# The modulation's row sums on VectorE at their written place in its queue, handed out over the scan and the first MLP

## The chip, the cores and the metric

One Trainium2 chip, and the program runs on 1 of its cores. The metric is the device time of one execution, in microseconds. A core has five engines with a queue each: TensorE (PE, with the weight loads shown as PEld), VectorE (DVE), ScalarE (ACT), GpSimd (POOL), and SyncE (SP), which here only issues transfers. Each queue is worked off in its order; an instruction that waits holds everything behind it in its own queue.

## The reference

A diffusion backbone of two layers over 256 context tokens and 1024 latent tokens, model width 1024. Layer 0 mixes with differential attention beside a bidirectional RWKV-7 recurrence; layer 1 with two other recurrences. What the change touches is the modulation: each layer makes six vectors of 1024 from the conditioning, for the latent tokens and for the context tokens, and uses them around the mixer and around the MLP.

```python
for i in range(DEPTH):
    ...
    m_l = (jax.nn.silu(c) @ mod_w + mod_b)[:, None, :]
    m_c = jax.nn.silu(c_ctx) @ mod_w + mod_b
    ...

def _ada(x, g, shift, scale):
    return rmsnorm(x, g) * (1.0 + scale) + shift

def _sq_relu_mlp(h, w1, w2):
    return jnp.square(jax.nn.relu(h @ w1)) @ w2
```

The six pieces of `m_l` and `m_c` are the shift, scale and gate of the mixer (`sh1`, `sc1`, `g1`) and of the MLP (`sh2`, `sc2`, `g2`). `mod_w` is 1024 x 6144. The vectors made in the stretches below are needed late: `g1` to `g2` of layer 0 after its scan, and layer 1's six not before the end of the first MLP.

## The kernel before

The activations lie with the model width on the 128 partitions: 8 blocks of 128 rows by 1280 tokens. A matrix product of full accuracy is three matmuls (`mm3`, L83 to L85) of a high and a low part of each operand: a weight tile comes in as `wraw`, ScalarE rounds it to `whi` (L91) and GpSimd makes `wlo` (L95).

The stages in order: first normalisation and modulation; the projections of layer 0 with the preparation of the RWKV operands; the **scan** of the RWKV recurrence; the attention heads; the output projection; the **first MLP**; then layer 1 and the second MLP.

**The row sums.** `mods_dot` makes modulation vectors without TensorE. For each vector and each of its 8 blocks of 128 outputs it loads the 128 x 1024 transposed weights (`mdw`, 512 KB, issued on SP at L212, two buffers) and lets VectorE multiply them by the row `silu_r` and add up along the row (L215; `mdj` takes the products, the sum lands in a column of `g1`, `sh2` and so on). Such an instruction is called a dot here. Vectors that the context needs too take two dots for each load. The generator yields after every second load, so a step is 2 loads with 4 dots, or with 2. The scan is handed a generator of 4 vectors with both rows: 16 steps, 32 loads, 64 dots. The first MLP is handed one of 6 vectors, two of them with both rows: 24 steps, 48 loads, 64 dots.

**The scan.** `Rwkv.scan` works through 10 windows of 128 tokens, both directions at once. In each turn `q` of a window it advances several generators by one piece: `window` (the two steps of the recurrence), `back` of the next window (the values and the inverse of the score blocks) and `front` of the window after that (scores and their masks), and hands out a step of the row sums where `q % 3 == 0`. The names in the rows: PE makes scores from `rkr` and `rbk` (L564), VectorE masks them into `rs` (L569), GpSimd cuts blocks out into `imb` (L571). `imc` (L616), shuffles to `imr` (L620), and a chain of products `ipr` (L627) and sums `iuc` (L628) on VectorE invert 8 x 8 blocks; GpSimd writes them to `id` (L632). Then `itt` is a transpose on VectorE (L648, L665), PE multiplies (L652, L658, L672, L683), and VectorE copies results back into `id` under a mask (L660). `iu` (L688) is the finished inverse. The recurrence's step goes PE (L705), `rpm` on VectorE (L708), PE (L711), `sav` on ScalarE and VectorE (L714, L715), PE (L720), the state `S` on VectorE (L724, L725). The projected operands `rkr` and `rbk` are loaded through SP (L553, L554).

**The first MLP.** `up(j)` makes one 128-wide tile of the hidden layer: PE into a bank of PSUM, `relu` on ScalarE (L339), its square on GpSimd (L340), `hidh` and `hidl` on VectorE (L93, L95). `down(c)` multiplies two such tiles by `w2` and adds the result to `x` on VectorE (L364), out of 4 banks `sp` and `ss`. The first three tiles are made in a loop of their own (`first`).

**The order.** The program is written in one order, and the framework's scheduler rearranges each engine's queue when the program is built, by a simulated timeline of its own. So the place of a dot in VectorE's queue need not be that at which it was handed out.

Of the kernel before, what the change touches and what calls it, by code (L numbers as in the profile page):

```python
# [8 lines left out]
F32 = mybir.dt.float32  # L9
# [3 lines left out]
ALU = mybir.AluOpType  # L13
AX = mybir.AxisListType
P = 128
# [11 lines left out]
class Net:  # L27
# [13 lines left out]
    def frame(self, nctx, nt):  # L41

        self.nctx, self.nt = nctx, nt

    @contextmanager
    def pools(self, **kw):
# [151 lines left out]
    def mods_dot(self, pool, rows, bufs, modt, modb, which, names, ctx):  # L198

        nc = self.nc
        outs = [self.const.tile([P, 8, 2], F32, name=nm) for nm in names]

        def steps():
            for (t0, w), o, both in zip(which, outs, ctx):
                if not both:
                    nc.gpsimd.memset(o[:, :, 1:2], 0.0)
                for t in range(8):  # L210
                    raw = pool.tile([P, 1024], F32, name="mdw", tag="mdw", bufs=bufs)
                    nc.sync.dma_start(out=raw, in_=modt[t0 + t])  # L212
                    for j in range(1 + both):
                        junk = pool.tile([P, 1024], F32, name="mdj", tag="mdj", bufs=1)
                        nc.vector.tensor_tensor_reduce(out=junk, in0=raw, in1=rows[:, j], scale=1.0, scalar=modb[:, 8 * w + t : 8 * w + t + 1],  # L215
                                                       op0=ALU.mult, op1=ALU.add, accum_out=o[:, t, j : j + 1])
                    if t % 2:
                        yield
        return outs, steps()
# [104 lines left out]
    def mlp(self, pool, xs, h, w1, w2, gate, groups, aside=iter(()), after=None, wide=None):  # L324


        nc = self.nc
# [41 lines left out]
        for gs in (groups[:-1], groups[-1:]):  # L369
            for w, evict in first:  # L370
                self.proj(w, h, gs, evict)
                next(aside, None)
        for c in range(NH // 2):
            if 0 < c < NH // 2 - 1:
                up(2 * c + 2)
# [7 lines left out]
class Rwkv:  # L383
# [366 lines left out]
    def scan(self, pool, aside):  # L750


        self.pool = pool
        self.half, self.posts = set(), []
        os = [{} for _ in range(12)]
        for g in (self.front(0, os[0]), self.back(os[0]), self.front(1, os[1])):
            for _ in g:
                pass
        self.start(pool)
        for sw in range(10):  # L760
            turn = [self.window(sw, os[sw])] + [self.back(os[sw + 1])] * (sw < 9) + [self.front(sw + 2, os[sw + 2])] * (sw < 8) + self.posts
            self.posts = []
            for q in count():
                turn = [g for g in turn if next(g, 0) is None]
                if not turn:
                    break
                if q % 3 == 0:
                    next(aside, None)

    def post(self, pool, w, d, y, tag):  # L770
# [1142 lines left out]
```

## Time and profile before

| | us |
|---|---|
| median of 3 runs | 4025.93 (4023.85 to 4026.64) |
| the profiled execution, its own time | 4028.34 |
| its span in the trace | 4026.6 |
| granted TensorE clock, mean | 0.929 |

The span is what the trace covers from the first to the last instruction. The clock is given as a share of TensorE's full speed. In the trace every line is that of the kernel before; in the changed kernel the same lines stand 4 further down (dots L220, `rpm` L712).

### The profile page before, as it was taken

To read this page: it belongs to the slowest core of one execution; us is meant where nothing else is said; L and a number is where in the kernel's file an instruction comes from. 1 tells how busy PE (TensorE), PEld (TensorE's weight loads), DVE (VectorE), ACT (ScalarE), POOL (GpSimd) and SP (SyncE) were. 2 spreads that over 40 slices of the span, in tenths; PEclk is the share of its full clock that TensorE was granted. 3 is DMA by queue.
4 is the path that set the end of the run, shared out by engine and by line. 5 is a ranking of instruction groups with operands and counts; after the bars stand their busy time and mean duration, and the time that the engine had idled before them with its cause. 6 is when DMAs were issued, how large, how long until landed. Compare 5 with 4: busy or idle time off the path is not lost. (4 is left out here: it accounts for less than half of the span.)

```text
span 4026.6 us, 69041 instructions
## 1 busy us (share of the span) xinstructions
PE 3604.7 (90%) x28912; PEld 2984.2 (74%) x28912; DVE 2066.0 (51%) x3741; ACT 1139.8 (28%) x1926; POOL 1315.4 (33%) x1121
## 2 busy tenths in 40 slices
PE   6999944777778889899999999999999889999998
PEld 4877833666666667778888887878776777888886
DVE  6354458555567647963333345457237664333335
ACT  3333320121245505111111112574534141111112
POOL 2455532222320015322222223216434353233223
PEclk8999975788889988999999999999989789999999
DMA  5244464223262142541111112222343311111111
GB/s 196 78 132 129 116 207 129 79 81 95 60 190 79 50 144 78 168 136 32 37 42 42 38 36 83 61 84 76 103 126 97 105 51 53 42 53 47 48 42 63
DMA packets 288998, 353.14 MB, mean 88 GB/s; under 512 B 91824, under 2 KB 217264, under 8 KB 288560
## 3 DMA queue, kind: packets, MB, share of 16 engines
q1 hardware_dynamic: 288688, 348.74, 27.8%
q8 instruction: 227, 3.72, 0.4%
q14 instruction: 83, 0.68, 0.0%
HBM read 265.03 MB, written 83.62 MB: 87 GB/s over the span
## 5 line engine op out<-in xcount | busy, mean ns | idle before, releaser
L83 PE MATMUL mm<-acth,whi 128*128 128x512 f32 (+1 forms) x2432 | 903.7, 373 | 26.6 <-ACT acth L91 6.9
L84 PE MATMUL mm<-actl,whi 128*128 128x512 f32 (+1 forms) x2432 | 905.2, 372 | 20.3 <-DVE actl L293 10.7
L85 PE MATMUL mm<-acth,wlo 128*128 128x512 f32 (+1 forms) x2432 | 894.4, 370 | 0.0
L95 POOL TENSOR_TENSOR wlo<-wraw,whi 128x1024 fp32r<-128x1024 f32 (+2 forms) x243 | 500.9, 2067 | 1036.6 <-ACT whi L91 1024.4
L83 PEld LDWEIGHTS mm<-acth,whi 128*128 128x128 f32 x2432 | 467.6, 193 | 122.5 <-issue 8.1
L84 PEld LDWEIGHTS mm<-actl,whi 128*128 128x128 f32 x2432 | 467.5, 192 | 109.0 <-DVE actl L293 11.8
L85 PEld LDWEIGHTS mm<-acth,wlo 128*128 128x128 f32 x2432 | 466.1, 192 | 83.0 <-issue 4.4
L91 ACT CAST whi<-wraw 128x1024 fp32r<-128x1024 f32 (+2 forms) x243 | 217.2, 906 | 994.8 <-PE mm L84 402.6
L340 POOL TENSOR_TENSOR relu<-relu 128x256 f32<-128x256 f32 (+1 forms) x163 | 162.0, 994 | 416.3 <-ACT relu L339 406.7
L93 DVE CAST hidh<-relu 128x256 fp32r<-128x256 f32 (+1 forms) x163 | 72.2, 443 | 366.0 <-POOL relu L340 365.7
L339 ACT ACTIVATE relu<-mm 128x256 f32<-128x256 f32 (+1 forms) x163 | 88.9, 546 | 591.5 <-PE mm L85 421.3
L84 PE MATMUL sp<-hidl,whi 128*128 128x512 f32 (+1 forms) x648 | 238.3, 368 | 1.5 <-DVE hidl L95 1.5
L83 PE MATMUL sp<-hidh,whi 128*128 128x512 f32 (+1 forms) x648 | 238.7, 369 | 0.9 <-DVE x L364 0.9
L85 PE MATMUL sp<-hidh,wlo 128*128 128x512 f32 (+1 forms) x648 | 238.1, 368 | 0.0
L83 PE MATMUL ss<-hidh,whi 128*128 128x512 f32 (+1 forms) x600 | 223.8, 373 | 4.7 <-DVE hidh L93 4.5
L84 PE MATMUL ss<-hidl,whi 128*128 128x512 f32 (+1 forms) x600 | 223.4, 372 | 4.9 <-DVE hidl L95 4.9
L85 PE MATMUL ss<-hidh,wlo 128*128 128x512 f32 (+1 forms) x600 | 222.8, 372 | 0.0
L215 DVE CUSTOM_DVE_ANT_0 mdj<-mdw,silu_r,t_cols 128x1024 f32<-128x1024 f32 x128 | 177.0, 1383 | 36.6 <-DMA mdw<-in_modt_dram 33.1
L364 DVE SCALAR_TENSOR_TENSOR x<-ss,g,x 128x256 f32<-128x256 f32 (+1 forms) x180 | 119.0, 661 | 140.6 <-PE ss L85 140.6
L364 DVE SCALAR_TENSOR_TENSOR x<-sp,g,x 128x512 f32<-128x512 f32 (+1 forms) x192 | 126.6, 660 | 101.7 <-PE sp L85 101.7
L364 DVE SCALAR_TENSOR_TENSOR x<-ss,g2b,x 128x512 f32<-128x512 f32 x120 | 90.0, 751 | 142.3 <-PE ss L85 142.3
L364 DVE SCALAR_TENSOR_TENSOR x<-sp,g2b,x 128x512 f32<-128x512 f32 (+1 forms) x132 | 96.7, 734 | 101.9 <-PE sp L85 101.9
(510 smaller groups left out, 6663.7 us busy)
## 6 DMA issues: line engine op xcount, KB each, us to landing
mdw<-in_modt_dram SPq DMA_DIRECT2D x80, 512.0 KB, 3.6
wraw<-in_wa_dram SPq DMA_DIRECT2D x64, 512.0 KB, 3.6
wraw<-in_wb_dram SPq DMA_DIRECT2D x64, 512.0 KB, 3.5
wraw<-in_win_dram SPq DMA_DIRECT2D x51, 512.0 KB, 3.7
x<-in_xT_dram SPq DMA_DIRECT2D x16, 640.0 KB, 8.5
rw_kr<-rw_t SPq DMA_DIRECT2D x16, 640.0 KB, 3.3
rw_bk<-rw_t SPq DMA_DIRECT2D x32, 320.0 KB, 4.1
rkr<-rw_kr SPq DMA_DIRECT2D x20, 512.0 KB, 5.9
```

The source lines that it names most:

```text
L83: self.nc.tensor.matmul(out, lh, rh, start=start and i == 0, stop=False)
L84: self.nc.tensor.matmul(out, lh, rl, start=False, stop=False)
L85: self.nc.tensor.matmul(out, ll, rh, start=False, stop=stop and i == n - 1)
L91: nc.scalar.copy(out=hi, in_=src)
L93: nc.vector.tensor_copy(out=hi, in_=src)
L95: e.tensor_tensor(out=lo, in0=src, in1=hi.bitcast(F32), op=ALU.subtract)
L215: nc.vector.tensor_tensor_reduce(out=junk, in0=raw, in1=rows[:, j], scale=1.0, scalar=modb[:, 8 * w + t : 8 * w + t + 1], op0=ALU.mult, op ...
L339: nc.scalar.activation(out=r, in_=ps, func=AF.Relu)
L340: nc.gpsimd.tensor_tensor(out=r, in0=r, in1=r, op=ALU.mult)
L364: nc.vector.scalar_tensor_tensor(out=xg, in0=ps, scalar=gate[:, m, j : j + 1], in1=xg, op0=ALU.mult, op1=ALU.add)
```

## The change

The dots are wrapped in `issue_after` of the last VectorE instruction written so far: the scheduler may no longer put a dot ahead of that instruction in VectorE's queue (there is no semaphore in it, only an order). The scan hands out a step where `q % 8 == 4`, which is twice in a window, in place of `q % 3 == 0`. The MLP hands out a step with each `up()` only, and none in the loop over the first three tiles.

```diff
--- before.py
+++ after.py
@@ -41,6 +41,10 @@
     def frame(self, nctx, nt):
 
         self.nctx, self.nt = nctx, nt
+
+    def last(self, engine):
+
+        return next(i for i in reversed(self.nc.cur_bb.bb.instructions) if i.engine == engine)
 
     @contextmanager
     def pools(self, **kw):
@@ -210,10 +214,11 @@
                 for t in range(8):
                     raw = pool.tile([P, 1024], F32, name="mdw", tag="mdw", bufs=bufs)
                     nc.sync.dma_start(out=raw, in_=modt[t0 + t])
-                    for j in range(1 + both):
-                        junk = pool.tile([P, 1024], F32, name="mdj", tag="mdj", bufs=1)
-                        nc.vector.tensor_tensor_reduce(out=junk, in0=raw, in1=rows[:, j], scale=1.0, scalar=modb[:, 8 * w + t : 8 * w + t + 1],
-                                                       op0=ALU.mult, op1=ALU.add, accum_out=o[:, t, j : j + 1])
+                    with self.tc.issue_after(self.last(mybir.EngineType.DVE)):
+                        for j in range(1 + both):
+                            junk = pool.tile([P, 1024], F32, name="mdj", tag="mdj", bufs=1)
+                            nc.vector.tensor_tensor_reduce(out=junk, in0=raw, in1=rows[:, j], scale=1.0, scalar=modb[:, 8 * w + t : 8 * w + t + 1],
+                                                           op0=ALU.mult, op1=ALU.add, accum_out=o[:, t, j : j + 1])
                     if t % 2:
                         yield
         return outs, steps()
@@ -369,7 +374,6 @@
         for gs in (groups[:-1], groups[-1:]):
             for w, evict in first:
                 self.proj(w, h, gs, evict)
-                next(aside, None)
         for c in range(NH // 2):
             if 0 < c < NH // 2 - 1:
                 up(2 * c + 2)
@@ -764,7 +768,7 @@
                 turn = [g for g in turn if next(g, 0) is None]
                 if not turn:
                     break
-                if q % 3 == 0:
+                if q % 8 == 4:
                     next(aside, None)
 
     def post(self, pool, w, d, y, tag):
```

**VectorE at the start of the scan.** Before, in the chain of products and sums of the first inverse (a dot is a row `ISA mdj`, the small `ISA` row behind it reads its sum out):

```order
L215 ISA mdj,g_4226<-mdw,silu_r,t_cols_66 128x1024
L215 ISA g_4226 128x1
L627 TENSOR_TENSOR ipr<-iuc,imr 128x16x2
L215 ISA mdj,g_4226<-mdw,silu_r,t_cols_66 128x1024
L215 ISA g_4226 128x1
L628 TENSOR_REDUCE iuc<-ipr 128x16
L215 ISA mdj,g_4226<-mdw,silu_r,t_cols_66 128x1024
L215 ISA g_4226 128x1
L627 TENSOR_TENSOR ipr<-iuc,imr 128x16x3
L215 ISA mdj,g_4226<-mdw,silu_r,t_cols_66 128x1024
L215 ISA g_4226 128x1
L628 TENSOR_REDUCE iuc<-ipr 128x16
```

After, the same chain:

```order
L631 TENSOR_TENSOR ipr<-iuc,imr 128x16x2
L632 TENSOR_REDUCE iuc<-ipr 128x16
L631 TENSOR_TENSOR ipr<-iuc,imr 128x16x3
L632 TENSOR_REDUCE iuc<-ipr 128x16
L631 TENSOR_TENSOR ipr<-iuc,imr 128x16x4
L632 TENSOR_REDUCE iuc<-ipr 128x16
L631 TENSOR_TENSOR ipr<-iuc,imr 128x16x5
```

The dots between the chain's steps are gone from here; no dot stands ahead of the scan's first `rpm`.

**VectorE in a window of the scan, between the last scores and the second step's `rpm`.** Before, behind the last two `rs`:

```order
L569 TENSOR_TENSOR rs_5327<-rw,t_masks_85 128x512
L569 TENSOR_TENSOR rs_5330<-rw,t_masks_85 128x512
L708 TENSOR_TENSOR rpm<-rbv,rw 128x512
L660 COPY_PREDICATED id<-t_masks_85,rw 128x16x16
L665 STREAM_TRANSPOSE itt<-id 128x512
L715 TENSOR_SCALAR sav_4365<-rw 64x512
L677 TENSOR_SCALAR iwt<-rw 32x512
```

After:

```order
L573 TENSOR_TENSOR rs_5303<-rw,t_masks_85 128x512
L573 TENSOR_TENSOR rs_5306<-rw,t_masks_85 128x512
L220 ISA mdj,g_4226<-mdw,silu_r,t_cols_66 128x1024
L220 ISA g_4226 128x1
L220 ISA mdj,g_4226<-mdw,silu_r,t_cols_66 128x1024
L220 ISA g_4226 128x1
L712 TENSOR_TENSOR rpm<-rbv,rw 128x512
L220 ISA mdj,g_4226<-mdw,silu_r,t_cols_66 128x1024
L220 ISA g_4226 128x1
L220 ISA mdj,g_4226<-mdw,silu_r,t_cols_66 128x1024
L220 ISA g_4226 128x1
```

Two dots moved in ahead of `rpm`, and two between `rpm` and the masked copy into `id` and its transpose.

**VectorE in the same window, the chain of the inverse.** Before, from `iu` on, and at the chain's end:

```order
L688 COPY iu<-rw 32x16x32
L627 TENSOR_TENSOR ipr<-iuc,imr 128x16x3
L628 TENSOR_REDUCE iuc<-ipr 128x16
L627 TENSOR_TENSOR ipr<-iuc,imr 128x16x4
L628 TENSOR_REDUCE iuc<-ipr 128x16
```

```order
L627 TENSOR_TENSOR ipr<-iuc,imr 128x16x6
L628 TENSOR_REDUCE iuc<-ipr 128x16
L627 TENSOR_TENSOR ipr<-iuc,imr 128x16x7
L628 TENSOR_REDUCE iuc<-ipr 128x16
L627 TENSOR_TENSOR ipr<-iuc,imr 128x128
L628 TENSOR_REDUCE iuc<-ipr 128x16
L648 STREAM_TRANSPOSE itt<-id 128x512
L708 TENSOR_TENSOR rpm<-rbv,rw 128x512
```

After, the same two places:

```order
L692 COPY iu<-rw 32x16x32
L220 ISA mdj,g_4226<-mdw,silu_r,t_cols_66 128x1024
L220 ISA g_4226 128x1
L631 TENSOR_TENSOR ipr<-iuc,imr 128x16x3
L220 ISA mdj,g_4226<-mdw,silu_r,t_cols_66 128x1024
L220 ISA g_4226 128x1
L632 TENSOR_REDUCE iuc<-ipr 128x16
```

```order
L220 ISA g_4226 128x1
L632 TENSOR_REDUCE iuc<-ipr 128x16
L631 TENSOR_TENSOR ipr<-iuc,imr 128x16x5
L632 TENSOR_REDUCE iuc<-ipr 128x16
L631 TENSOR_TENSOR ipr<-iuc,imr 128x16x6
L632 TENSOR_REDUCE iuc<-ipr 128x16
L631 TENSOR_TENSOR ipr<-iuc,imr 128x16x7
L632 TENSOR_REDUCE iuc<-ipr 128x16
L712 TENSOR_TENSOR rpm<-rbv,rw 128x512
L631 TENSOR_TENSOR ipr<-iuc,imr 128x128
L632 TENSOR_REDUCE iuc<-ipr 128x16
L652 STREAM_TRANSPOSE itt<-id 128x512
```

Four dots moved in between `iu` and the chain's second sum from there, and `rpm` moved up ahead of the chain's last product and sum and of the transpose `itt`. Eight windows out of the ten have a group of four dots at the one place, and eight at the other.

**VectorE in the first MLP.** Before, near the start of the MLP, among the operands of the first hidden tiles (`act` is the normalised input):

```order
L215 ISA mdj,sh1b<-mdw,silu_r,t_cols_68 128x1024
L215 ISA sh1b 128x1
L95 TENSOR_TENSOR hidl<-relu,hidh 128x512
L215 ISA mdj,sh1b<-mdw,silu_r,t_cols_68 128x1024
L215 ISA sh1b 128x1
L293 TENSOR_TENSOR actl<-adat,acth 128x512
L215 ISA mdj,sh1b<-mdw,silu_r,t_cols_68 128x1024
L215 ISA sh1b 128x1
L93 CAST hidh<-relu 128x256
```

After, the dots handed out first stand further on, among the additions to `x` of the first `down()`:

```order
L99 TENSOR_TENSOR hidl<-relu,hidh 128x512
L220 ISA mdj,sh1b<-mdw,silu_r,t_cols_68 128x1024
L220 ISA sh1b 128x1
L369 SCALAR_TENSOR_TENSOR x_14437<-ss,g_4229,x_14437 128x512
L220 ISA mdj,sh1b<-mdw,silu_r,t_cols_68 128x1024
L220 ISA sh1b 128x1
L369 SCALAR_TENSOR_TENSOR x_14437<-sp,g_4229,x_14437 128x512
L369 SCALAR_TENSOR_TENSOR x_14438<-ss,g_4229,x_14438 128x256
L220 ISA mdj,sh1b<-mdw,silu_r,t_cols_68 128x1024
L220 ISA sh1b 128x1
L369 SCALAR_TENSOR_TENSOR x_14438<-sp,g_4229,x_14438 128x512
```

A dot now stands behind each of a few additions, four with a step; later steps have two.

On SP the loads of `mdw` moved with the dots: 2 behind the scan's preparation, then in each window two ahead of the loads of `rbk` and `rkr`, one behind them and one further on; in the MLP two behind each weight tile. On the other engines the order is the same but for single instructions.

## Rows read from the trace of the kernel before

**Rows 1.** The page: the span; busy time of each engine with its share of the span and its instructions; the dots as the page groups them (busy us, mean ns | idle time of VectorE just before them, and what ended most of it).

```profile
span 4026.6 us, 69041 instructions
PE 3604.7 (90%) x28912; PEld 2984.2 (74%) x28912; DVE 2066.0 (51%) x3741; ACT 1139.8 (28%) x1926; POOL 1315.4 (33%) x1121
L215 DVE CUSTOM_DVE_ANT_0 mdj<-mdw,silu_r,t_cols 128x1024 f32<-128x1024 f32 x128 | 177.0, 1383 | 36.6 <-DMA mdw<-in_modt_dram 33.1
```

**Rows 2.** The dots by their tile: shortest, median and longest in ns, and the start of the first and of the last in us.

```profile
L215 DVE CUSTOM_DVE_ANT_0 mdj<-mdw,silu_r,t_cols x128: 1237/1284/3412, 549.3 to 1768.1; 128x1024 f32<-128x1024 f32 x128
```

**Rows 3.** Busy time by stretch (us from the span's start): length; busy us and instructions of PE, PEld, DVE, ACT, POOL; granted clock; DMA share; GB/s. The first is from the first dot of the scan to its first `rpm`, the second lies in it; the third is the scan's first window and the fourth a later one, each from an `rpm` to the same one of the next window; the last two lie in the first MLP.

```profile
549.34:678.05 128.71, 43.52 (x956) 37.41 (x954) 99.55 (x175) 9.98 (x17) 29.89 (x25) 0.59 0.62 194
600.00:650.00 50.00, 9.93 (x573) 9.22 (x575) 43.59 (x78) 1.19 (x2) 6.67 (x5) 0.50 0.52 163
678.05:739.39 61.34, 37.40 (x1104) 33.66 (x1104) 36.33 (x96) 8.22 (x14) 12.51 (x17) 0.69 0.20 63
876.59:921.13 44.54, 33.02 (x1104) 29.75 (x1104) 22.87 (x54) 8.18 (x14) 9.50 (x14) 0.81 0.23 74
1600.00:1800.00 200.00, 180.40 (x864) 149.15 (x863) 166.20 (x247) 28.03 (x38) 61.89 (x34) 0.95 0.47 150
1800.00:2000.00 200.00, 200.00 (x1036) 170.15 (x1035) 76.40 (x129) 25.24 (x36) 56.07 (x38) 1.00 0.14 43
```

**Rows 4.** The dots alone in the first and third of these stretches: length; busy us and count on VectorE; clock; DMA share; GB/s.

```profile
549.34:678.05 128.71, 77.60 (x59) 0.59 0.62 194
678.05:739.39 61.34, 6.48 (x5) 0.69 0.20 63
```

**Rows 5.** VectorE's timeline at the start of the scan: start, duration, line, operation, tiles, and in brackets the idle time before it and what ended it.

```profile
581.09 1.28 DVE L215 CUSTOM_DVE_ANT_0 mdj<-mdw,silu_r,t_cols 128x1024 f32<-128x1024 f32 x1 [11.51 <-DMA mdw<-in_modt_dram]
586.60 1.98 DVE L616 TENSOR_REDUCE imc<-imb 128x128 f32<-128x1024 f32 x1 [0.61 <-POOL imb L571]
...
617.98 0.70 DVE L648 STREAM_TRANSPOSE itt<-id 128x512 f32<-128x512 f32 x1
...
631.35 0.42 DVE L660 COPY_PREDICATED id<-t_masks,rw 128x256 f32<-128x256 int32 x1
...
646.00 0.42 DVE L660 COPY_PREDICATED id<-t_masks,rw 128x256 f32<-128x256 int32 x1
...
678.05 0.68 DVE L708 TENSOR_TENSOR rpm<-rbv,rw 128x512 f32<-128x512 f32 x1
```

**Rows 6.** PE's timeline there: the products whose results the two masked copies take, and the last product of that inverse.

```profile
623.41 1.81 PE L658 MATMUL rw<-id,iwt 32*32 32x32 f32 x115 [1.44 <-issue]
...
637.05 1.81 PE L658 MATMUL rw<-id,iwt 32*32 32x32 f32 x115 [0.33 <-issue]
...
651.04 0.31 PE L683 MATMUL rw<-id,iwt 32*32 32x32 f32 x2 [0.74 <-ACT iwt L679]
```

**Rows 7.** VectorE's timeline in the later window, one without dots.

```profile
897.27 1.29 DVE L569 TENSOR_TENSOR rs<-rw,t_masks 128x512 f32<-128x512 f32 x2 [4.92 <-PE rw L564]
898.48 0.68 DVE L708 TENSOR_TENSOR rpm<-rbv,rw 128x512 f32<-128x512 f32 x1
...
902.01 0.44 DVE L660 COPY_PREDICATED id<-t_masks,rw 128x256 f32<-128x256 int32 x1 [2.85 <-PE rw L658]
902.48 0.71 DVE L665 STREAM_TRANSPOSE itt<-id 128x512 f32<-128x512 f32 x1
...
908.59 2.02 DVE L616 TENSOR_REDUCE imc<-imb 128x128 f32<-128x1024 f32 x1 [1.11 <-POOL imb L571]
...
918.20 0.27 DVE L628 TENSOR_REDUCE iuc<-ipr 128x16 f32<-128x112 f32 x1
...
920.39 0.71 DVE L648 STREAM_TRANSPOSE itt<-id 128x512 f32<-128x512 f32 x1 [1.27 <-POOL id L632]
921.13 0.69 DVE L708 TENSOR_TENSOR rpm<-rbv,rw 128x512 f32<-128x512 f32 x1
...
924.60 0.69 DVE L715 TENSOR_SCALAR sav<-rw 64x512 f32<-64x512 f32 x1 [1.58 <-ACT sav L714]
```

**Rows 8.** PE's timeline in that window: what stands behind the transpose of 902.48, behind the `rpm` of 921.13 and behind the `sav` of 924.60.

```profile
903.53 1.20 PE L672 MATMUL rw<-itt,rs 32*32 32x32 f32 x64
...
921.97 1.65 PE L711 MATMUL rw<-rpm,iu 64*64 64x64 f32 x26 [3.58 <-DVE rpm L708]
...
926.26 0.48 PE L720 MATMUL rw<-sav,rbt 128*64 128x64 f32 x2
```

**Rows 9.** GpSimd's timeline: a pair of blocks cut out at the start of the scan, with dots on VectorE, and in the later window, without.

```profile
583.06 3.50 POOL L571 TENSOR_TENSOR imb<-rs,t_masks 64x256 f32<-64x256 f32 x2 [12.47 <-DVE rs L569]
...
898.04 1.52 POOL L571 TENSOR_TENSOR imb<-rs,t_masks 64x256 f32<-64x256 f32 x2 [8.38 <-DVE rs L569]
```

**Rows 10.** What PE waited for from 1590 to 1770 us, the first stretch of the first MLP: us in total, times, longest.

```profile
PE mm L83 <- ACT relu L339: 5.0, 3, 3.1
PE ss L84 <- DVE hidl L95: 4.9, 2, 2.7
PE ss L83 <- DVE hidh L93: 4.5, 1, 4.5
```

**Rows 11.** SP's timeline and PE's in the later window: the loads of `rkr` for the window after next, and the scores that read them.

```profile
909.30 1.04 SPq L553 DMA_DIRECT2D rkr<-rw_kr  x2
...
916.30 2.08 PE L564 MATMUL rw<-rkr,rbk 64*128 64x128 f32 x16 [0.72 <-DVE iuc L628]
```

## The prediction, made before the changed kernel was run

> **What bounds the kernel now.** The page first: PE is busy for 90% of the span and VectorE for 51%, and all 128 dots together take 177 us of VectorE [rows 1]. So in most of the program VectorE's work lies beside PE's, and a dot's place can matter only where PE waits. The dots' own range, 549 to 1768 us [rows 2], says where to look, and the table by stretch shows two such places. At the start of the scan, from the first dot to the first `rpm`, PE is busy for 43.5 of 128.7 us while VectorE is busy for 99.6 [rows 3], 77.6 of them with 59 dots [rows 4]. In the first MLP PE loses 19.6 of the first 200 us, at a clock of 0.95, and then nothing at all at 1.00 [rows 3]. Between the two lies the scan, where a later window takes 44.5 us with PE busy for 33.0, VectorE for 22.9 and GpSimd for 9.5: there no engine is full, and the time is that of a chain that goes back and forth between PE and VectorE. So the reader should see two stretches in which the bunches of dots stand in the way, and, between them, windows now free of dots that will get eight each.
>
> **The change part by part.** The order shows the dots out of the scan's start, in two groups of four in each of eight windows, and in the MLP behind the first hidden tiles. Work is neither added nor removed. A dot takes 1.28 us in the median [rows 2] and 1.38 in the mean [rows 1]; I use 1.30 where nothing is in its way.
>
> *The start of the scan.* Four pieces of the one chain of the first inverse.
> (a) VectorE stood for 11.51 us until 581.09 for a dot's load, with masked scores queued behind it, and the dot took 1.28 [rows 5]: 12.8 goes.
> (b) From `imc` to the first `itt` took 31.4 us (586.60 to 617.98), with a dot between nearly all steps [rows 5]; the same chain took 11.8 in the later window (908.59 to 920.39) [rows 7]: 19.6 goes.
> (c) PE had the results for the two masked copies at 625.22 and 638.86 [rows 6], VectorE took them at 631.35 and 646.00 [rows 5]. The copies were 6.1 and 7.1 late, in a queue of dots; in the later window the copy waited for PE [rows 7]: 13.3 goes.
> (d) From the last product of the inverse at 651.04 [rows 6] to the first `rpm` at 678.05 [rows 5] is 27.0 us with 13 dots, 17 at 1.30 each. What part PE's own work covers the rows don't tell. Nothing goes at the least, 17 at the most; I take 9, half.
> The sum is −55. Bounds: −46 without (d), −63 with the whole of it.
>
> *The scan's first window.* It has 5 dots at its head, 6.5 us [rows 4], and takes 16.8 us more than the later one; 4.4 of that is PE's own work being slower (37.4 against 33.0 busy, clock 0.69 against 0.81) [rows 3], which may stay. The other 12.4 goes: −12, bounds −6.5 (the dots alone) and −16.8. Its new group of dots is counted next.
>
> *The windows.* No window of before has dots in these places, so I walk through the later one.
> First group: two dots ahead of the second step's `rpm`, two behind it. Masked scores end at 898.5; two dots put `rpm` at 901.1, and two more, to 904.4, the copy that now goes at 902.01 after 2.85 us of waiting [rows 7]. PE's next product, at 903.53 [rows 8], moves with the transpose: +2.4.
> Second group: four dots, 5.2 us, in the chain of the inverse. The sum at 918.20 ends at 923.7, and `rpm`, now directly behind it, goes there and not at 921.13; then come the last product and sum, GpSimd's 1.27, the transpose, and `sav`, at about 927.6 and not at 924.60 [rows 7]. PE waits for that `rpm` already (3.58) and for `sav` behind it [rows 8]. Between the 2.5 of `rpm` and the 3.0 of `sav` I take 2.5.
> With the 0.1 by which the mean dot is above the median for each of eight dots that makes 5.7 a window, and +46 for eight. Bounds: +19 if only one group costs its 2.4, +83 if each dot costs its 1.30.
> One thing in the trace bears on that 0.1: a pair of cuts on GpSimd took 3.50 us beside dots and 1.52 without [rows 9], so the two engines are in each other's way. [...]
>
> *The MLP.* Its first 200 us lose 19.6 in idle time, and the clock of 0.95 costs 5% of 180.4, 9.0: 28.6 in all [rows 3]. PE waited there 4.9 for `hidl` and 4.5 for `hidh`, VectorE's work behind dots, and 5.0 for `relu` on ScalarE [rows 10]. The `relu` wait is not the dots', and I leave 5 for it. The new places cost something too: the 64 dots go over some hundreds of us in which PE now waits for nothing and VectorE is busy for 38% [rows 3], beside additions that have PSUM banks to spare, so nothing for most; I put 5, four dots that meet a hidden tile. −18, bounds −4 (9.4 for `hidl` and `hidh`, less 5) and −28.6.
>
> *SP.* A load of `mdw` now stands ahead of the loads of `rkr` in each window. A dot of the first group frees its buffer by 904.4, and `rkr` goes out at 909.30 behind a load that waits for PE: nothing, with the price in the rivals.
>
> Sum: −55 −12 +46 −18 = −39. The profiled execution took 4028.3, so 3989; it lay 2.4 above the median, so **3987**.
>
> **The rivals.** A measurement of this kernel can tell about 0.2%, 8 us, from no change.
> *A, the dots hide in the scan too.* For it: VectorE is idle for half of a window. Against: PE waits for `rpm` directly behind the dots [rows 8]. One us a window, the MLP keeping 25: −55 −12 +8 −25 = −84, 3942.
> *B, each dot costs its own time in the windows.* For it: the scan is one chain, and both groups stand on it. Against: the first copy has 2.85 us of slack. With +83 the sum is −2, 4024; with the scan's start at its lower bound too, 4033.
> *C, the other side: the clock.* PE's clock follows how busy it is: 0.50 where PE worked 9.9 of 50 us, 0.69 in the slow first window, 0.81 in the later ones, 1.00 in the full MLP [rows 3]. If windows with dots fall to the first one's state, each takes 16.8 more, +134 over eight: −55 −12 +134 −18 = +49, 4075. It decides from 11 us a window. Against it: a window 6 us longer is nearer to 44.5 than to 61.3, and keeps PE's gaps about as short. [...]
> *D, the loads.* `rkr` is issued at 909.30 and read from 916.30 on [rows 11], with little to spare. If the loads of `mdw` ahead of it hold it back by that whole distance, 7.0 a window, that is +56 and a sum of +17, 4043. Against it: the buffers are free 5 us earlier.
> That the change moves nothing is excluded by the order.
>
> **How the numbers follow.** Chances: the forecast 0.68, A 0.10, B 0.14, C 0.05, D 0.03. The forecast's own range is 3954 to 4018, from about half of each bound taken together. The range of 3945 to 4030 holds it, the upper half of A and most of B; what it leaves out is half of A, C, D and the end of B, 0.17. Faster (below 4018) has the forecast, A and a fifth of B: 0.81. Same has three fifths of B: 0.09. Slower has C, D and the rest: 0.10.
>
> **What would show it.** In the changed kernel the first `rpm` comes some 55 us earlier, near 623, and the first masked copies go when PE's product ends. Windows with dots take about 50 us at a clock of at least 0.77, with PE waiting longer for `rpm` and for the transposes; about 45 would be A, 55 B, 60 at 0.70 C. PE's waits for `rkr` would stand out under D. In the MLP the waits for `hidh` and `hidl` are gone, and PE stays above 195 of 200 us after the first hidden tiles. The prediction is wrong if a window costs 10 us or more, or if the scan's start keeps its length because the loads of `rkr`, PE's slow clock or GpSimd set it in place of the dots.

## The result and the profile of the changed kernel

The changed kernel takes 3971.7 us in the median of 4 runs (3967.53 to 3980.13), the kernel before in the same comparison 4024.9: a ratio of 0.9873, with a 95% interval of 0.9853 to 0.9894. That is 53 us less, where 38 were forecast (3987, range 3945 to 4030). The same kernel came to 3970.4 and 3966.1 in two later comparisons, 56 and 59 below the kernel before on the same chip.

The page first: the span (61 less than in [rows 1], since the profiled execution of before lay 2.4 above its median and this one 4.2 below), and the dots, whose wait for a load is gone. (In the changed kernel the lines from the dots to the first MLP stand 5 further down, not 4: the dots at L220, `relu` at L344.)

```profile
span 3965.7 us, 68983 instructions
L220 DVE CUSTOM_DVE_ANT_0 mdj<-mdw,silu_r,t_cols 128x1024 f32<-128x1024 f32 x128 | 172.7, 1349 | 1.2
```

The dots by their tile, as in [rows 2]: they now run from 645 to 2275 us, and not from 549 to 1768.

```profile
L220 DVE CUSTOM_DVE_ANT_0 mdj<-mdw,silu_r,t_cols x128: 1271/1280/2014, 644.9 to 2274.7; 128x1024 f32<-128x1024 f32 x128
```

Busy time by stretch, with the columns of [rows 3]: from the same instant to the first `rpm`; the scan's first window; the second, the fourth and the fifth; and the first MLP's first two stretches of 200 us.

```profile
549.34:617.65 68.31, 39.15 (x958) 34.13 (x956) 25.30 (x57) 10.20 (x18) 16.73 (x25) 0.68 0.48 143
617.65:671.68 54.03, 34.71 (x1104) 31.16 (x1104) 38.30 (x100) 8.22 (x14) 10.76 (x15) 0.78 0.27 87
671.68:724.00 52.32, 35.61 (x1104) 32.08 (x1104) 33.83 (x70) 8.21 (x14) 13.85 (x16) 0.76 0.42 129
777.29:830.90 53.61, 34.01 (x1106) 30.47 (x1104) 36.38 (x79) 8.22 (x14) 12.08 (x15) 0.82 0.39 126
830.90:879.01 48.11, 32.48 (x1104) 29.29 (x1104) 32.66 (x70) 8.18 (x14) 10.36 (x14) 0.85 0.36 112
1545.00:1745.00 200.00, 199.39 (x1020) 169.93 (x1020) 113.42 (x192) 43.97 (x64) 60.32 (x43) 0.97 0.17 51
1745.00:1945.00 200.00, 200.00 (x1033) 169.90 (x1032) 103.39 (x176) 26.46 (x38) 60.77 (x39) 1.00 0.27 85
```

Three things are to be seen. The scan's start takes 68.3 us and not 128.7, with nearly the same work on PE (39.2 against 43.5 busy, at a higher clock). The windows, 44.5 in the one of [rows 3], are now 48 to 54. And PE is full at the beginning of the MLP, busy for 199.4 of 200 us where it had 180.4, although VectorE still has dots there in the second stretch (103 busy against 76).

VectorE at the start of the scan, to be held against [rows 5]: no dot, and the instructions wait for PE instead of being waited for.

```profile
574.40 1.98 DVE L620 TENSOR_REDUCE imc<-imb 128x128 f32<-128x1024 f32 x1 [1.04 <-POOL imb L575]
...
584.82 0.71 DVE L652 STREAM_TRANSPOSE itt<-id 128x512 f32<-128x512 f32 x1 [1.20 <-POOL id L636]
590.76 0.42 DVE L664 COPY_PREDICATED id<-t_masks,rw 128x256 f32<-128x256 int32 x1 [5.23 <-PE rw L662]
...
597.60 0.43 DVE L664 COPY_PREDICATED id<-t_masks,rw 128x256 f32<-128x256 int32 x1 [5.68 <-PE rw L662]
...
617.65 0.68 DVE L712 TENSOR_TENSOR rpm<-rbv,rw 128x512 f32<-128x512 f32 x1
```

PE there, as in [rows 6]:

```profile
588.40 2.31 PE L662 MATMUL rw<-id,iwt 32*32 32x32 f32 x128 [0.80 <-ACT iwt L657]
...
601.76 0.31 PE L687 MATMUL rw<-id,iwt 32*32 32x32 f32 x2 [0.74 <-ACT iwt L683]
```

VectorE in the fifth window, which answers to [rows 7]: first the group of dots around the second step's `rpm`, then the one in the chain of the inverse, up to the next window's `rpm`.

```profile
850.85 1.37 DVE L220 CUSTOM_DVE_ANT_0 mdj<-mdw,silu_r,t_cols 128x1024 f32<-128x1024 f32 x1
...
852.26 1.62 DVE L220 CUSTOM_DVE_ANT_0 mdj<-mdw,silu_r,t_cols 128x1024 f32<-128x1024 f32 x1
...
853.82 0.68 DVE L712 TENSOR_TENSOR rpm<-rbv,rw 128x512 f32<-128x512 f32 x1
...
856.94 0.44 DVE L664 COPY_PREDICATED id<-t_masks,rw 128x256 f32<-128x256 int32 x1
857.42 0.71 DVE L669 STREAM_TRANSPOSE itt<-id 128x512 f32<-128x512 f32 x1
...
871.09 0.69 DVE L692 COPY iu<-rw 32x512 f32<-32x512 f32 x1
871.81 1.28 DVE L220 CUSTOM_DVE_ANT_0 mdj<-mdw,silu_r,t_cols 128x1024 f32<-128x1024 f32 x1
...
878.71 0.27 DVE L632 TENSOR_REDUCE iuc<-ipr 128x16 f32<-128x112 f32 x1
879.01 0.69 DVE L712 TENSOR_TENSOR rpm<-rbv,rw 128x512 f32<-128x512 f32 x1
```

What PE waited for in the scan from the first to the last `rpm` (617 to 1089 us), the two lines that changed most (total, times, longest):

```profile
PE rw L715 <- DVE rpm L712: 49.0, 14, 6.9
PE rw L676 <- DVE itt L669: 15.2, 8, 2.6
```

The same wait for `rpm` in the kernel before, from 678 to 1118 us:

```profile
PE rw L711 <- DVE rpm L708: 30.0, 8, 5.1
```

The product of L676 (L672 there) has no wait for the transpose `itt` in that kernel. So the windows pay at the places of the walk: at `rpm`, and at the transpose behind the first group's dots.

Where the 61 us between the two profiled executions lie, by the marks in the traces (first and last `rpm`, the first `relu`, the MLP's first and last product with `hidh`, the second MLP's last one):

| stretch, us | before | changed | difference | forecast |
|---|---|---|---|---|
| start to the first `rpm` | 678.1 | 617.6 | −60.4 | −55 |
| first to last `rpm` of the scan | 440.2 | 471.9 | +31.6 | −12 +46 = +34 |
| to the first MLP's first `relu` | 451.5 | 456.4 | +4.9 | 0 |
| first `relu` to the end of the first MLP | 933.9 | 905.0 | −28.9 | −18 |
| layer 1 with the second MLP | 1498.8 | 1490.6 | −8.2 | 0 |

### The profile page after: what moved, and what is told of

It reads as the page before. It is cut to its first block, busy times and chain, and to the rows that moved or that the text cites. A ratio compares the mean times of both kernels' runs of the same rounds, so it can differ in the third digit from the quotient of the medians.

```text
span 3965.7 us, 68983 instructions
## 1 busy us (share of the span) xinstructions
PE 3587.8 (90%) x28912; PEld 2976.9 (75%) x28912; DVE 2048.2 (52%) x3741; ACT 1138.8 (29%) x1926; POOL 1305.6 (33%) x1121
## 4 chain that ended last, share of the span: by engine, by line
PE 58%; DVE 3%; DMA 1%; ACT 1%; issue 1%; POOL 0%; SPq 0%; POOLq 0%; ACTq 0%; DVEq 0%
PE mm L87 10%; PE mm L88 10%; PE mm L89 10%; PE ss L87 4%; PE ss L88 4%; PE ss L89 4%; PE sp L88 4%; PE sp L87 4%; PE sp L89 4%; PE sp L1222 1%; PE ss L1475 1%; PE sp L1406 1%; PE si L1491 1%; PE mm L1232 1%; DMA wraw<-in_wout_dram 0%
## 5 line engine op out<-in xcount | busy, mean ns | idle before, releaser
L344 ACT ACTIVATE relu<-mm 128x256 f32<-128x256 f32 (+1 forms) x163 | 88.9, 545 | 520.8 <-PE mm L89 378.7
L369 DVE SCALAR_TENSOR_TENSOR x<-ss,g,x 128x256 f32<-128x256 f32 x180 | 118.9, 661 | 145.2 <-PE ss L89 145.2
L220 DVE CUSTOM_DVE_ANT_0 mdj<-mdw,silu_r,t_cols 128x1024 f32<-128x1024 f32 x128 | 172.7, 1349 | 1.2
## 6 DMA issues: line engine op xcount, KB each, us to landing
x<-in_xT_dram SPq DMA_DIRECT2D x16, 640.0 KB, 10.7
```

What stands on the lines that cost most here:

```text
L344: nc.scalar.activation(out=r, in_=ps, func=AF.Relu)
L369: nc.vector.scalar_tensor_tensor(out=xg, in0=ps, scalar=gate[:, m, j : j + 1], in1=xg, op0=ALU.mult, op1=ALU.add)
```

## The experiments

The theory: the bunches cost at the scan's start and in the MLP what the chain of the first inverse and the hidden tiles waited for them; the windows pay for what the dots add to the waits of the chain between PE and VectorE; the three add up. The rivals: each dot costs its own time wherever it stands, the windows' longer time is not the dots' but the clock's or the loads', or one part is the whole gain.

One part of the change needs no run. With the new rates alone, without the order edge, the scheduler builds the queues of all five engines row by row as those of before: the rates by themselves do nothing.

**The scan's part alone.** The MLP keeps its old hand-outs and has no edge.

```diff
-    def mods_dot(self, pool, rows, bufs, modt, modb, which, names, ctx):
+    def mods_dot(self, pool, rows, bufs, modt, modb, which, names, ctx, pin=True):
...
-                    with self.tc.issue_after(self.last(mybir.EngineType.DVE)):
+                    with self.tc.issue_after(self.last(mybir.EngineType.DVE)) if pin else nullcontext():
...
             for w, evict in first:
                 self.proj(w, h, gs, evict)
+                next(aside, None)
...
+                ("sh1b", "sc1b", "g1b", "sh2b", "sc2b", "g2b"), (True, True, False, False, False, False), pin=False)
```

> The scan's dots as in the changed kernel, the first MLP's as before. The two profiles put the scan's start at -60.4 (first rpm at 617.65 and not 678.05) and the rest of the scan at +31.6 (first to last rpm 471.9 and not 440.3). Sum theory (the parts add up): 29 below the kernel before, about 3996, with the first MLP's idle time unchanged. Rival, the change of the MLP is the whole gain, and the scan gives back what it gained: within 8 of the kernel before. Rival, the scan alone makes the whole gain and the MLP only moves with the clock: 53 below.

Measured: 4005.6, 21 below the kernel before (ratio 0.9946, 0.9926 to 0.9967), 8 short of the theory's 29, which lies within the interval (13 to 30 below). The profiled execution is its fastest, 3992.8; there the first `rpm` is at 616.4, the scan takes 475.0, and the MLP 932.7 as before, so that the scan's part is 27. Both rivals fall: it is neither nothing nor the whole.

**The MLP's part alone.** The same flag at the scan's call, and `q % 3 == 0` there.

> The first MLP's dots as in the changed kernel, the scan's as before. Sum theory: 29 below the kernel before (first relu to the MLP's last product 933.2 us before and 904.3 after in the two profiles), about 3996; PE busy above 208 of the first 210 us. Rival: the MLP's part is that of the start only, 19.6 us of idle time, with the clock unchanged: 15 to 20 below.

Measured: 3991.2, 35 below (0.9915, 0.9896 to 0.9934). The scan is as before (first `rpm` at 681.5, then 440.0), and the MLP takes 903.7 and not 933.9. The two parts come to 21 + 35 = 56 where the whole change has 53 to 59: they add up. The rival with the start alone falls, since the MLP is 30 shorter and not 15 to 20.

**A kernel that was to have no dots in the scan.**

> The changed kernel without the 64 dots and 32 loads of the scan: layer 0's g1, sh2, sc2 and g2 are left at zero, so the output is another. It prices the dots at their new places. Sum theory (the walk through a window, 5 to 6 us for eight dots): 40 to 46 below the changed kernel, about 3928, windows of 45 us. Rival, each dot costs its own 1.30 us: 83 below, about 3889. Rival, they hide: within 10 of the changed kernel, 3962 or more.

The edit added an argument that nothing read, so this was the changed kernel once more, with all its dots. It prices nothing; as a repetition it gave 3970.4, with 471.7 from first to last `rpm`.

**The scan without its dots.**

```diff
         outs = [self.const.tile([P, 8, 2], F32, name=nm) for nm in names]
+        if skip:
+            for o in outs:
+                nc.gpsimd.memset(o, 0.0)
+            return outs, iter(())
```

> The changed kernel without the 64 dots and 32 loads of the scan (layer 0's g1, sh2, sc2 and g2 stay zero, so the output is another). The scan from its first to its last rpm took 440 before, 472 in the changed kernel and 447 with the four places. Sum theory: the windows lose 40 to 46 to the changed kernel and the first one is near the others without its old 5 dots, so 426 to 432 from first to last rpm, and 40 to 46 less time than the changed kernel. Rival, each dot costs its own 1.30 us in the chain: 83 less, 389. Rival, the dots are hidden in the changed kernel and its longer windows come from another cause, the clock or the loads: 465 or more.

Measured: 3925.8 (0.9750 of before, 0.9735 to 0.9765), 40 to 46 less than the changed kernel's 3966 to 3972. From first to last `rpm` it takes 429.8. So the 64 dots with their 32 loads cost 42.0 us, where the dots themselves are 83 long, in the changed kernel's windows; PE's waits for the loads of `rkr` there are 1.3 to 4.6 us in three profiles of that kernel, so the loads themselves hold PE up by little. Against the kernel before it is 10.4 less (440.2 to 429.8), and that is the first window without its old 5 dots: 50.2 and not 61.3. Both rivals fall. What the 42.0 is made of is seen in the same table by stretch, first to last `rpm`, without dots:

```profile
619.30:1049.10 429.80, 312.59 (x10175) 277.24 (x10176) 234.57 (x600) 87.45 (x158) 112.31 (x142) 0.85 0.25 75
```

and in the changed kernel:

```profile
617.65:1089.50 471.85, 329.16 (x10176) 294.12 (x10176) 317.80 (x730) 87.70 (x159) 127.17 (x145) 0.79 0.33 102
```

The same 10,176 matmuls are busy for 16.6 us longer at a clock of 0.79 and not 0.85; the other 25.4 is idle time of PE. So some two fifths of the price is matmuls that take longer at a lower clock. The idle time is at the two places named above: without dots PE waits for `rpm`

```profile
PE rw L719 <- DVE rpm L716: 31.8, 8, 5.0
```

which is 17 less than in the changed kernel, and the 15.2 for the transpose is gone; the two are more than the 25.4, since other waits are shorter with the dots. The price is uneven: window by window the first eight take 1.3 to 9.2 us more with dots than without, and the fifth, whose timeline is shown above, is the cheapest.

**Four other places in the window.** Two dots at a time, in the first four turns of each of eight windows.

```diff
-                    if t % 2:
+                    if (t + 1) % every == 0:
                         yield
...
+                                                  [(8 * q, 2 + q) for q in range(4)], ("g1", "sh2", "sc2", "g2"), (True,) * 4, every=1)
...
-                if q % 8 == 4:
+                if q in (0, 1, 2, 3):
                     next(aside, None)
```

> The changed kernel with the scan's dots handed out two at a time, in the first four turns of a window. The order then has them at four places, behind the masked scores, behind sav, ahead of the masked copy and at the first transpose, where VectorE waited for PE for 1.6 to 4.9 us in a window without dots, and none in the chain of the inverse. Theory, a dot costs what it adds to PE's wait for rpm, and nothing in a wait of VectorE: windows of 46 to 48 us, 20 to 35 below the changed kernel, about 3945. Rival, the window pays for VectorE's time wherever it stands: within 8 of the changed kernel. Rival, the loads of mdw ahead of rkr hold up the scores: above the changed kernel, with PE waiting for a load.

Measured: 3936.9 (0.9780, 0.9760 to 0.9799), 33 below the changed kernel beside it; 3938.9 when it was repeated on another chip (0.9789, 0.9768 to 0.9810). It is faster than both kernels of this study. The scan takes 447.1 from first to last `rpm`: the 64 dots cost 17.3 us and not 42.0. PE waits for no load of `rkr` there, so both rivals fall. The stretch in the columns of the table above:

```profile
617.43:1064.49 447.06, 324.85 (x10175) 289.71 (x10176) 321.14 (x728) 87.26 (x158) 127.90 (x142) 0.80 0.35 108
```

Against the kernel without dots PE is idle for only 5.0 us more (122.2 and 117.2); the other 12.3 is its matmuls at 0.80 and not 0.85. VectorE's timeline in a window of it, from the first step's `rpm` to the second's and the next window's:

```profile
908.13 0.69 DVE L712 TENSOR_TENSOR rpm<-rbv,rw 128x512 f32<-128x512 f32 x1
...
909.94 1.37 DVE L220 CUSTOM_DVE_ANT_0 mdj<-mdw,silu_r,t_cols 128x1024 f32<-128x1024 f32 x1
...
911.35 1.63 DVE L220 CUSTOM_DVE_ANT_0 mdj<-mdw,silu_r,t_cols 128x1024 f32<-128x1024 f32 x1
...
913.74 1.28 DVE L220 CUSTOM_DVE_ANT_0 mdj<-mdw,silu_r,t_cols 128x1024 f32<-128x1024 f32 x1
...
920.46 1.63 DVE L220 CUSTOM_DVE_ANT_0 mdj<-mdw,silu_r,t_cols 128x1024 f32<-128x1024 f32 x1
...
922.02 0.41 DVE L664 COPY_PREDICATED id<-t_masks,rw 128x256 f32<-128x256 int32 x1
922.35 1.27 DVE L220 CUSTOM_DVE_ANT_0 mdj<-mdw,silu_r,t_cols 128x1024 f32<-128x1024 f32 x1
...
932.32 0.69 DVE L712 TENSOR_TENSOR rpm<-rbv,rw 128x512 f32<-128x512 f32 x1 [0.56 <-PE rw L709]
...
953.44 0.69 DVE L712 TENSOR_TENSOR rpm<-rbv,rw 128x512 f32<-128x512 f32 x1
```

This window has eight dots (three of them left out here) and takes 45.3 us, 0.8 more than the one without any in [rows 3]; it is one of the shorter ones, the eight take 45.2 to 53.3, on average 48.7, where 46 to 48 was expected. The second `rpm` waits for PE (0.56), so the dots ahead of it have lost nothing that counts; the chain of the inverse behind it has no dot, and so the next `rpm` comes 21.1 later (22.7 in [rows 7]). That bears the theory out as far as waits go: the 64 dots add 5.0 us to PE's idle time in places where VectorE waits for PE, and 25.4 in the places of the changed kernel, where PE waits for VectorE. The last pair, at the first transpose, is the weak place: PE's waits for that transpose are 13.9, and 5.7 without dots, which shorter waits elsewhere make good in part.

**The edge with the old rates.** `q % 3 == 0` in the scan and the hand-outs in the MLP's first loop put back, the edge kept.

> Dots kept at their written place, but handed out at the old rates: all 64 of the scan in its first three windows, about 20 a window, and those of the MLP from its first tiles on. Theory, VectorE's waits in a window take some 8 dots and the rest lies on the chain: three windows cost 55 to 75 us together, the scan's start stays at 617, the MLP gains 20 to 29; sum 10 to 35 below the kernel before, 15 to 45 above the changed kernel. Rival, the rates make no difference once the place is kept: within 8 of the changed kernel.

Measured: 3987.9 (0.9911, 0.9893 to 0.9929), 40 below the kernel before, a little more than the 10 to 35 expected, and 16 to 22 above the changed one. The first `rpm` is at 615.5, so the start needs the edge alone; the scan takes 487.7, 57.9 more than without dots, 57 of it in its first three windows, within the 55 to 75 forecast. The MLP takes 913.9. The rates matter once the place is kept.

**The hand-outs in the MLP's first loop put back**, in the changed kernel otherwise.

```diff
             for w, evict in first:
                 self.proj(w, h, gs, evict)
+                next(aside, None)
```

> The changed kernel with the hand-outs in the loop over the MLP's first three tiles put back: six steps, 24 dots, 31 us of VectorE in the 50 us in which PE first waits for hidden tiles. Theory, these dots stand ahead of hidh and hidl: from the first relu to the first down 53 to 60 and not 50, the whole 3 to 10 above the changed kernel. Rival, VectorE has the time: within 3 by the stretch, no difference in the whole.

Measured: 3985.0 and, on the chip of the changed kernel's repetition, 3979.1; both are 13 above the changed kernel, more than the 3 to 10 expected, and the runs are scattered (3971 to 4001, and 3969 to 3992). In the profile of the repetition the stretch to the first `down` is 53.5 and not 50.1, the rest of the MLP 862.3 and not 855.0, and PE waits at its beginning for a hidden tile (1540 to 1760 us):

```profile
PE ss L87 <- DVE hidh L97: 5.9, 1, 5.9
```

In the changed kernel that wait was 0.4 (1545 to 1755 us):

```profile
PE ss L87 <- DVE hidh L97: 0.4, 1, 0.4
PE ss L88 <- DVE hidl L99: 0.2, 1, 0.2
```

So dropping these hand-outs is worth 10.7 by the stretches, and 7.9 in the first profile (51.6 and 861.4).

**A second choice of places.** As the four, with turn 4 in the place of turn 3.

```diff
-                if q in (0, 1, 2, 3):
+                if q in (0, 1, 2, 4):
```

> As the four places, with the fourth pair not ahead of and behind the first transpose but ahead of the second step's rpm. In the four places a half window from the first to the second rpm took 26.1 and not 24.0: sav is late by about 1.0 behind the first pair, and the transpose by 1.3 behind a dot. Theory: the second of these goes, and rpm has 3 us to spare at its new neighbour: 1.0 and not 2.3 a window, 8 to 12 below the four places, about 437 from first to last rpm. Rival, the dots ahead of rpm are on the chain: 2.6 a window in the place of 1.3, 10 above the four places.

Measured: 3954.9 (0.9821, 0.9805 to 0.9838). The scan is the shorter by 4.3, 442.8, less than the 8 to 12 forecast, and for another reason. The wait for the first transpose did shrink, from

```profile
PE rw L656 <- DVE itt L652: 13.9, 7, 4.8
```

with the four places to

```profile
PE rw L656 <- DVE itt L652: 8.5, 6, 4.8
```

but other waits grew, and PE's idle time as a whole is 5.3 longer (127.5 and 122.2). What makes the scan shorter is the matmuls, 9.5 us less at a clock of 0.83 and not 0.80:

```profile
615.82:1058.62 442.80, 315.35 (x10175) 280.58 (x10176) 324.55 (x728) 87.73 (x159) 134.54 (x142) 0.83 0.35 109
```

Yet the whole is 18 longer than with the four places. The excess lies outside the scan, where the two kernels' code is the same. Four kernels on one chip, each run in 5 rounds, were to settle that.

> The changed kernel once more, on one chip with the next three. Both theories below: 50 to 56 below the kernel before.

> The four places once more. Their scan is 4 longer than with the second choice of places (447 and 443 from first to last rpm), but the whole was 18 shorter in another call, 11 of it between the scan and the first MLP (448 and 459) and 8 in layer 1 (1494 and 1502). Theory, the scheduler lays out the attention heads and layer 1 anew whenever a queue ahead of them changes, and its layout here costs less: the whole again 14 to 20 shorter than the second choice, the two stretches again near 448 and 1494. Rival, the chip or the execution: within 6 of the second choice, with the stretches alike.

> The second choice of places once more, beside the four places. Layout theory: 14 to 20 longer than those, 459 between scan and MLP, 1502 in layer 1. Rival, the chip or the execution: within 6 of them, or shorter by the scan's 4.

> The kernel with the hand-outs in the loop over the first tiles once more. TensorE's queue in layer 1 is row by row that of the four places, and yet layer 1 took 1512 and not 1494. Layout theory alone would have 1494 here too, and the whole 8 above the changed kernel by the MLP's 855 to 861 and 50.0 to 51.6. Rival, that stretch varies from execution to execution whatever the order: again away from 1494 by more than 8, or spread by 20 over the rounds.

Measured: 3966.1 (59 below the kernel before), 3938.9, 3955.5 and 3979.1. The second choice is again 17 longer than the four places, on another chip, so the rival of the chip falls for these two. In the four places, repeated, the last `rpm` and the first `relu` are

```profile
L712 DVE TENSOR_TENSOR rpm<-rbv,ry x2: 686/686/687, 1045.0 to 1065.7; 128x512 f32<-128x512 f32 x2
...
L344 ACT ACTIVATE relu<-mm x163: 361/592/602, 1514.4 to 3884.9; 128x512 f32<-128x512 f32 x125, 128x256 f32<-128x256 f32 x38
```

and in the second choice

```profile
L712 DVE TENSOR_TENSOR rpm<-rbv,ry x2: 687/687/687, 1048.2 to 1064.8; 128x512 f32<-128x512 f32 x2
...
L344 ACT ACTIVATE relu<-mm x163: 361/592/601, 1522.5 to 3904.1; 128x512 f32<-128x512 f32 x125, 128x256 f32<-128x256 f32 x38
```

that is 448.7 and 457.7 between the two. TensorE's queue in the attention heads has one layout in the kernels before, with the MLP's part alone, without the dots and with the four places, or nearly so, and there the stretch took 448.2 to 451.5 in five profiles. The edge with the old rates has that layout too, and took 453.5. It has another in the changed kernel, with the scan's part alone, with the first loop kept and with the second choice, and there it took 453.0 to 459.2 in eight. So the scheduler lays out what follows anew when a queue ahead of it changes, and the two layouts lie some 6 us apart in the mean; that the order is the cause is likely, not shown, since no run changed it alone and one order spreads by 6 of itself.

In layer 1 the second choice took 1502.4 and 1504.9, the four places 1494.2 twice, the changed kernel 1487.2 to 1490.6 in three profiles. There it is not waits: PE is idle for 51 to 52 us in the second choice and for 55 with the four places, and its matmuls take 11 to 15 longer at 0.96 and not 0.97. And one order can do the same: the kernel with the first loop kept, which has the four places' order on TensorE in layer 1, took 1512.4 in one profile and 1489.8 in the other, 20 of the 23 in the matmuls (1457.3 and 1436.9 busy, clock 0.954 and 0.968). What sets the clock there stays open, and so whether the layout counts in layer 1.

## Why the prediction was right, and where it was off

**The place of the loss and of the price.** All four terms have the sign that the walk through the rows gave, and three nearly the size: −60.4 for −55, −10.4 for −12, +42.0 for +46, −28.9 for −18. The sum of the measured four is −57.7, of the forecast four −39; most of the difference is the MLP's 11.

**The scan's start.** (a) `imc` comes at 574.40 and not at 586.60: 12.2 for 12.8. (b) From `imc` to the first transpose is 10.4 and not 31.4: 21.0 for 19.6. (c) The first masked copy starts at 590.76, when PE ends at 590.71, and both copies wait 5.2 to 5.7 for PE; from the transpose to the second copy it is 12.8 and not 28.0, 15.2 for 13.3; the clock has no part in it, it is 0.50 in both stretches with PE busy for 8.4 and 8.3 us. (d) From PE's last product to `rpm` it is 15.9 and not 27.0: 11.1, where I took 9, half of the dots' 17. The half was a guess between 0 and 17, and it came near by luck: PE is busy for 15.1 of the 15.9, so its own work now covers that stretch, but 5.2 of the 11.1 is that work running at 0.72 and not 0.63, which the guess about the dots did not hold.

**The first window.** It falls by 11.1 without dots (61.3 to 50.2), where I took 12. But I let 4.4 of PE's slower work stay and took 12.4 of waiting away; 5.8 of the 11.1 is PE's matmuls (37.4 to 31.6 busy, clock 0.69 to 0.84) and 5.3 is idle time. The size is right by luck.

**The windows.** I walked through one of them and got 5.7; the price is 42.0 over eight, 5.3. In the fifth window the copy follows the dots directly (856.94) and PE's `rpm` waits grew from 30.0 to 49.0 over the scan, as the walk had it. What it didn't see is that 16.6 of the 42.0 is PE's matmuls, longer at a lower clock: it took all of the price for waiting, and 25.4 is. The forecast's size was right partly by luck, because the two errors, too much waiting and no clock, offset one another.

**The MLP, the term that was mis-sized.** Of 28.6 lost I left 5 to the `relu` wait, as "not the dots'", and put 5 for dots that would meet a hidden tile. Both were nothing: PE waits 0.4 and 0.2 in the first 210 us of the MLP in the changed kernel, and the new places lie all in the shadow of the additions. That the `relu` wait was an after-effect of VectorE's queue could be read before: ScalarE's `relu` itself waited there for `hidl` (1570 to 1770 us of the kernel before):

```profile
ACT relu L339 <- DVE hidl L95: 72.3, 15, 8.6
```

The term came out at the end of its range, as the whole loss: over the MLP PE is idle for 19.6 us less, and its matmuls take 9.2 less at a clock of 0.99 and not 0.98. That the hand-outs in the first loop were dropped is a part of it that I had not priced by itself: 8 to 11.

**The rivals.** A, dots that hide, is excluded for the changed places (42.0), and comes nearer with the four places (17.3, of which 5.0 is waiting). B, each at its own price, would have had 83. C was there in the small: the clock of the scan is 0.79 where it is 0.85 without dots, and the eight windows lie between 0.76 and 0.85, not at the 0.69 of the old first window. D did not come: PE's waits for `rkr` in the scan are 1.3, 3.6 and 4.6 us in three profiles of the changed kernel and were 5.1 before.

**What was not in the sum.** The text ahead of the prediction says that the other engines' order is the same but for single instructions. That nearly holds for the scan (161 of TensorE's 10,176 rows stand elsewhere), and not behind it: the layout of the heads changed, and the stretch to the MLP is 4.9 longer, layer 1 8.2 shorter in the profiled pair. I counted nothing there. The two nearly cancel in this kernel; in the second choice of places both are longer than with the four places, and took more than the scan gave.

**VectorE beside GpSimd.** In the fifth window the two dots that follow masked scores take 1.37 and 1.62, and the pair of cuts that GpSimd makes beside them 2.38 (from 850.42 on), where dots elsewhere take 1.28 and the pair took 1.52 without dots [rows 9]. Over the scan's 64 dots the mean is 0.09 above the median (1379 and 1285 ns), which is the 0.1 of the sum. It is the same in the whole scan: its eight pairs of cuts beside dots take 2.38 to 2.40, its pairs with no dot beside them 1.51 to 1.53 (in the fifth window 1.52, from 863.08 on); the 16 dots beside cuts take 1.37 and 1.62 to 1.63, the 9 beside other work of GpSimd 1.27 to 2.01, and the 39 with none of it beside them 1.27 to 1.28. So both get longer where they overlap; how that comes about, no run here shows.

## What to carry to other kernels

Work that only fills an engine has a price by its place and not by its length: 64 dots of 1.3 us cost 42 in one set of places in a window and 17 in another, and the timeline of a window without them shows which (where VectorE stood idle for PE, the 64 dots added 5.0 us to PE's idle time; ahead of instructions that PE waits for, 25.4). A bunch that a scheduler makes at build time has to be looked for in the trace and held apart with an order edge, and with a rate that fits the edge: the rate alone changed no queue, and the edge with the old rates was 16 to 22 us longer than the edge with the new. And after any such change the stages behind it must be measured too, since the scheduler lays them out anew: a stretch where nothing had been edited differed by up to 11 us between two kernels.

## What was not expected of the hardware

The clock had a part in nearly every difference of the scan, and it does not go by the sum of the waits. From first to last `rpm`, with the same 10,176 matmuls (a record is missing in some traces):

| kernel | PE busy, us | PE idle, us | granted clock |
|---|---|---|---|
| without dots | 312.6 | 117.2 | 0.85 |
| second choice of places | 315.4 | 127.5 | 0.83 |
| four places | 324.9 | 122.2 | 0.80 |
| changed kernel | 329.2 | 142.7 | 0.79 |

The second choice has 5.3 us more idle time than the four places and yet the higher clock, and it is so again in the repetitions of both (315.2 busy and 127.7 idle; 324.9 and 120.9). So no fixed price of clock goes with a microsecond of waiting here: 25.4 us of added idle time came with 16.6 of slower matmuls in the changed kernel, and 5.0 with 12.3 in the four places. Nor does the clock go by PE's busy share over the stretch, as rival C had it from one kernel's rows: PE is busy for 73% of it both without dots and with the four places, at 0.85 and 0.80. What sets the clock in the scan, no run here shows.
